# Rotary embedding on one core: runs of one position range side by side in neighbouring partitions, and nine transfers instead of ten

## The chip, the cores and the metric

The kernel runs on one core of one Trainium2 chip. The metric is the device time of an execution in microseconds, the lower the better.

## The reference

Batch 16, 512 positions, 16 heads of 64 numbers, all fp32: 33.55 MB in and as much out, both in HBM, the memory outside the core. Only the first 32 numbers of each head change.

```python
x1, x2 = x[..., :32], x[..., 32:]
cos, sin = cos[None, :, None, :], sin[None, :, None, :]     # from [512, 32]
first  = x1[..., :16] * cos[..., :16] - x1[..., 16:] * sin[..., :16]
second = x1[..., :16] * sin[..., :16] + x1[..., 16:] * cos[..., :16]
out = concatenate([first, second, x2], axis=-1)
```

## The kernel before

x is cut into four tiles of four batches. A tile has 128 partitions (the rows of the on-chip memory), and each partition holds a run of K = 16 positions, 64 KiB in one piece. The on-chip ring holds three tiles, so load 3 must wait until store 0 has emptied its slot. All large transfers are issued by SyncE into one queue, in program order. Partition p holds run p of the tile's four batches in memory order, that is position range p mod 32, so the small tables (32 ranges) are copied four times.

```python
    xf = x.rearrange("b s h d -> (b s h d)").rearrange("(t p f) -> t p f", t=T, p=P)
    ...
    def load(t, lo=0, hi=K):
        nc.sync.dma_start(out=rows(t, lo, hi), in_=xf[t, :, lo * R : hi * R])
    ...
    nc.gpsimd.dma_start(out=stage[:, 0].rearrange("p k j -> p (k j)"), in_=cosf)
    nc.gpsimd.dma_start(out=stage[:, 1].rearrange("p k j -> p (k j)"), in_=sinf)
    load(0, 0, K0)          # K0 = 4 rows
    load(0, K0, K)
    load(1)
    load(2, 0, KC)          # KC = 8 rows
    for r in range(REP):    # REP = 4
        nc.vector.tensor_copy(out=table[r * PB : (r + 1) * PB]..., in_=stage...)
    ...
    def rotate(t, lo, hi):  # four VectorE instructions on rows lo to hi
        ...
    rotate(0, 0, K0)
    rotate(0, K0, (K0 + K) // 2)
    rotate(0, (K0 + K) // 2, K)
    store(0)
    load(2, KC, K)
    load(3)
    for t in range(1, T):
        rotate(t, 0, KC)
        rotate(t, KC, K)
        store(t)
```

## Time and profile before

| | before |
|---|---|
| time, median | 161.92 us (161.79 to 162.01, 6 runs) |
| span in the profile | 160.1 us |
| VectorE busy | 110.0 us |
| large transfers' queue | 97.8% of 16 engines' span |

The span runs from the first to the last instruction. A share near 100% says that the 16 transfer engines always had work; idle time of VectorE costs nothing then. The main lines are in the prediction. An issue is the instruction that hands a transfer over; a transfer lands when the last of its 16 engines has reported.

### The profile page before, as it was taken

The page shows a single profiled execution, that of the slowest core. Times are in us where ns is not written, and L with a number is a line of the kernel's source. Part 1 is how long each engine was busy: PE and PEld are TensorE (multiplying, and loading weights), DVE is VectorE, ACT ScalarE, POOL GpSimd, SP SyncE. Part 2 cuts the span into 40 slices and gives each one's busy share as a digit, 9 for nine tenths or more (in the row PEclk, how much of TensorE's full clock was granted, in tenths as well). Part 3 has the DMA queues.
Part 4 walks back from the last instruction along what each step waited for, and adds up shares of the span by engine and source line. Part 5 has one row for each costly group of instructions (what it writes and reads, how often), then busy time and mean ns, then how long its engine had stood idle before and what let it go on. Part 6 is the DMA issues. An engine that isn't in the chain of part 4 may idle for free.

```text
span 160.1 us, 109 instructions
## 1 busy us (share of the span) xinstructions
DVE 110.0 (69%) x40; POOL 1.3 (1%) x6
## 2 busy tenths in 40 slices
DVE  0069709999999999999999994799999900000000
POOL 3000000000000000000000000000000000000000
DMA  6999999699699799899996996996996996996991
GB/s 197 385 504 454 393 459 524 262 524 491 295 401 581 328 524 409 377 393 418 483 540 295 491 524 262 524 524 262 524 524 262 524 524 262 524 491 295 524 459 66
DMA packets 1504, 67.24 MB, mean 420 GB/s; under 512 B 192, under 2 KB 192, under 8 KB 224
## 3 DMA queue, kind: packets, MB, share of 16 engines
q1 hardware_dynamic: 1440, 67.11, 97.8%
q0 software_dynamic: 64, 0.13, 0.2%
HBM read 33.69 MB, written 33.55 MB: 420 GB/s over the span
## 4 chain that ended last, share of the span: by engine, by line
DMA 50%; DVE 28%; DVEq 1%; issue 0%; SPq 0%
DMA ring<-in_x_dram 32%; DMA out_dram<-ring 18%; DVE b_t L83 10%; DVE ring L84 10%; DVE ring L85 5%; DVE ring L88 3%; DVEq L127 1%; SPq L53 0%; DVEq L83 0%
## 5 line engine op out<-in xcount | busy, mean ns | idle before, releaser
L83 DVE TENSOR_TENSOR b_t<-ring,table 128x4096 f32<-128x4096 f32 (+2 forms) x9 | 35.6, 3959 | 8.2 <-DMA ring<-in_x_dram 8.0
L84 DVE TENSOR_TENSOR ring<-ring,table 128x4096 f32<-128x4096 f32 (+2 forms) x9 | 35.6, 3950 | 0.3
L85 DVE TENSOR_TENSOR ring<-ring,b_t 128x2048 f32<-128x2048 f32 (+2 forms) x9 | 18.4, 2049 | 0.3
L88 DVE TENSOR_TENSOR ring<-ring,b_t 128x2048 f32<-128x2048 f32 (+2 forms) x9 | 18.4, 2042 | 0.0
L67 DVE COPY table<-stage 32x1024 f32<-32x1024 f32 x4 | 2.7, 684 | 9.2 <-DMA stage<-in_sin_dram 9.1
L58 POOL DMA_DIRECT2D stage<-in_cos_dram x1 | 0.6, 631 | 0.8 <-PEq L127 0.8
L59 POOL DMA_DIRECT2D stage<-in_sin_dram x1 | 0.5, 498 | 0.0
L116 POOL MEMSET const-bfloat16-1.0<- 128x1 bf16 x1 | 0.1, 102 | 0.0
L116 POOL MEMSET const-float32-0.0<- 128x1 f32 x1 | 0.1, 99 | 0.2 <-issue 0.2
L116 POOL MEMSET const-float32-1.0<- 128x1 f32 x1 | 0.1, 99 | 0.0
L116 POOL MEMSET const-uint8-127<- 128x1 uint8 x1 | 0.1, 99 | 0.0
## 6 DMA issues: line engine op xcount, KB each, us to landing
ring<-in_x_dram SPq DMA_DIRECT2D x2, 4096.0 KB, 43.9
ring<-in_x_dram SPq DMA_DIRECT2D x1, 6144.0 KB, 22.4
ring<-in_x_dram SPq DMA_DIRECT2D x1, 2048.0 KB, 8.5
stage<-in_cos_dram POOLq DMA_DIRECT2D x1, 64.0 KB, 6.0
stage<-in_sin_dram POOLq DMA_DIRECT2D x1, 64.0 KB, 7.2
out_dram<-ring SPq DMA_DIRECT2D x4, 36.4
ring<-in_x_dram SPq DMA_DIRECT2D x2, 35.0
```

Source lines behind the costliest of these rows:

```text
L58: nc.gpsimd.dma_start(out=stage[:, 0].rearrange("p k j -> p (k j)"), in_=cosf)
L59: nc.gpsimd.dma_start(out=stage[:, 1].rearrange("p k j -> p (k j)"), in_=sinf)
L67: nc.vector.tensor_copy(out=table[r * PB : (r + 1) * PB].rearrange("p t k c j -> p (t k) c j"), in_=stage.rearrange("p t k j -> p (t k) j" ...
L83: nc.vector.tensor_mul(out=b_t, in0=x1, in1=s)
L84: nc.vector.tensor_mul(out=x1, in0=x1, in1=c)
L85: nc.vector.tensor_sub(out=x1[:, :, :, 0:Q], in0=x1[:, :, :, 0:Q], in1=b_t[:, :, :, Q:HF])
L88: nc.vector.tensor_add(out=x1[:, :, :, Q:HF], in0=x1[:, :, :, Q:HF], in1=b_t[:, :, :, 0:Q])
L116: nc = _bacc.Bacc("TRN2", target_bir_lowering=False, num_devices=1)
L127: with _tile.TileContext(nc) as tc:
```

## The change

Partition 4j+b now holds range j of batch b. Four neighbouring partitions need the same table row, so one shuffle, whose mask names a source for each of 32 partitions, replaces the four copies. The transfers are regrouped: three whole loads, two stores, the last load in 7 and 9 rows, two stores.

```diff
-    xf = x.rearrange("b s h d -> (b s h d)").rearrange("(t p f) -> t p f", t=T, p=P)
+    xf = x.rearrange("(t b) (j k) h d -> t j b (k h d)", t=T, k=K)
     ... (of alike)
-        nc.sync.dma_start(out=rows(t, lo, hi), in_=xf[t, :, lo * R : hi * R])
+        nc.sync.dma_start(out=rows(t, lo, hi), in_=xf[t, :, :, lo * R : hi * R])
     ...
+    nc.vector.memset(stage[:, :, :, 0:Q], 0.0)
+    first = stage.rearrange("(j b) t k i -> j b t (k i)", b=REP)
+    nc.gpsimd.dma_start(out=first[:, 0, 0], in_=cosf)     # every fourth partition
     ...
-    load(0, 0, K0)
-    load(0, K0, K)
+    load(0)
     load(1)
-    load(2, 0, KC)
+    load(2)
-    for r in range(REP):
-        nc.vector.tensor_copy(...)
+    nc.vector.stream_shuffle(out=table..., in_=stage..., mask=[p // REP * REP for p in range(32)])
     ...
-    rotate(0, 0, K0)
-    rotate(0, K0, (K0 + K) // 2)
-    rotate(0, (K0 + K) // 2, K)
-    store(0)
-    load(2, KC, K)
-    load(3)
-    for t in range(1, T):
+    for t in range(NS - 1):
         rotate(t, 0, KC)
         rotate(t, KC, K)
         store(t)
+    load(NS, 0, KA)         # KA = 7
+    load(NS, KA, K)
+    for t in range(NS - 1, T):
+        cuts = [0, KC, K] if t < NS else [0, KA, (KA + K) // 2, K]
+        for lo, hi in zip(cuts, cuts[1:]):
+            rotate(t, lo, hi)
+        store(t)
```

More of the change, by code (lines that the diff above doesn't have):

```diff
@@ L33 @@
     KC = K // 2
-    K0 = K // 4
-    xf = x.rearrange("b s h d -> (b s h d)").rearrange("(t p f) -> t p f", t=T, p=P)
-    of = out.rearrange("b s h d -> (b s h d)").rearrange("(t p f) -> t p f", t=T, p=P)
+    KA = 7
+    xf = x.rearrange("(t b) (j k) h d -> t j b (k h d)", t=T, k=K)
+    of = out.rearrange("(t b) (j k) h d -> t j b (k h d)", t=T, k=K)
     cosf = cos.rearrange("(p k) j -> p (k j)", k=K)
@@ L45 @@
     ring = const_pool.tile([P, NS, K, H, D], fp32)
-    stage = const_pool.tile([PB, 2, K, HF], fp32)
+    stage = const_pool.tile([P, 2, K, HF], fp32)
     table = const_pool.tile([P, 2, K, 2, Q], fp32)
@@ L52, in load @@
     def load(t, lo=0, hi=K):
-        nc.sync.dma_start(out=rows(t, lo, hi), in_=xf[t, :, lo * R : hi * R])
+        nc.sync.dma_start(out=rows(t, lo, hi), in_=xf[t, :, :, lo * R : hi * R])
     def store(t, lo=0, hi=K):
-        nc.sync.dma_start(out=of[t, :, lo * R : hi * R], in_=rows(t, lo, hi))
-    nc.gpsimd.dma_start(out=stage[:, 0].rearrange("p k j -> p (k j)"), in_=cosf)
-    nc.gpsimd.dma_start(out=stage[:, 1].rearrange("p k j -> p (k j)"), in_=sinf)
-    load(0, 0, K0)
-    load(0, K0, K)
-    load(1)
-    load(2, 0, KC)
-    for r in range(REP):
-        nc.vector.tensor_copy(
-            out=table[r * PB : (r + 1) * PB].rearrange("p t k c j -> p (t k) c j"),
-            in_=stage.rearrange("p t k j -> p (t k) j")[:, :, 0:Q]
-            .unsqueeze(2)
-            .to_broadcast((PB, 2 * K, 2, Q)),
-        )
+        nc.sync.dma_start(out=of[t, :, :, lo * R : hi * R], in_=rows(t, lo, hi))
+    nc.vector.memset(stage[:, :, :, 0:Q], 0.0)
+    first = stage.rearrange("(j b) t k i -> j b t (k i)", b=REP)
+    nc.gpsimd.dma_start(out=first[:, 0, 0], in_=cosf)
+    nc.gpsimd.dma_start(out=first[:, 0, 1], in_=sinf)
+    load(0)
+    load(1)
+    load(2)
+    nc.vector.stream_shuffle(
+        out=table.rearrange("p t k c j -> p (t k) c j"),
+        in_=stage.rearrange("p t k j -> p (t k) j")[:, :, 0:Q]
+        .unsqueeze(2)
+        .to_broadcast((P, 2 * K, 2, Q)),
+        mask=[p // REP * REP for p in range(32)],
+    )
     C = table[:, 0].rearrange("p k c j -> p k (c j)")
@@ L76, in rotate @@
     def rotate(t, lo, hi):
-        n = hi - lo
         x1 = ring[:, t % NS, lo:hi, :, 0:HF]
-        c = C[:, lo:hi].unsqueeze(2).to_broadcast((P, n, H, HF))
-        s = Sn[:, lo:hi].unsqueeze(2).to_broadcast((P, n, H, HF))
+        c = C[:, lo:hi].unsqueeze(2).to_broadcast((P, hi - lo, H, HF))
+        s = Sn[:, lo:hi].unsqueeze(2).to_broadcast((P, hi - lo, H, HF))
         b_full = b_pool.tile([P, KC, H, HF], fp32, name="b_t")
-        b_t = b_full[:, 0:n]
+        b_t = b_full[:, 0 : hi - lo]
         nc.vector.tensor_mul(out=b_t, in0=x1, in1=s)
```

## The prediction

> **What bounds the kernel now.** I read the page first, its parts 1 to 3. In this page the columns are shares of the span or, in the rows of digits, tenths busy in 40 slices of 4 us.
>
> ```profile
> span 160.1 us, 109 instructions
> DVE 110.0 (69%) x40; POOL 1.3 (1%) x6
> DVE  0069709999999999999999994799999900000000
> DMA  6999999699699799899996996996996996996991
> q1 hardware_dynamic: 1440, 67.11, 97.8%
> HBM read 33.69 MB, written 33.55 MB: 420 GB/s over the span
> ```
>
> The reader is to see that VectorE is busy for 69% and the transfers for 97.8 + 0.2%. The queue moved 67.11 MB in 0.978 x 160.1 = 156.6 us, or 429 GB/s while it worked. Each byte of x is read once and each byte of the output written once, so no change of layout makes the bytes fewer. The slices with 6 are an effect of counting large packets where they end, as longer windows show.
>
> Next, windows longer than a packet (columns: window, its length, VectorE busy, POOL busy, clock, DMA share, GB/s), and three short ones at the two ends.
>
> ```profile
> 54.00:100.00 46.00, 43.59 (x14) 0.00 (x0) 1.00 1.00 433
> 2.00:158.00 156.00, 110.01 (x40) 0.38 (x1) 1.00 1.00 430
> 1.00:1.50 0.50, 0.00 (x0) 0.25 (x1) 1.00 0.00 0
> 1.50:2.00 0.50, 0.00 (x0) 0.50 (x2) 1.00 2.12 459
> 159.00:159.50 0.50, 0.00 (x0) 0.00 (x0) 1.00 0.00 0
> ```
>
> From 2 to 158 us the share is 1.00: there is no hole to fill. What lies outside is the start (first bytes between 1.5 and 2.0 us, for a load issued at 0.74) and about 1.5 us at the end.
>
> Third, the time from issue to landing of single transfers, which I asked for in narrow windows, and the chain of waits from store 0 on.
>
> ```profile
> ring<-in_x_dram SPq DMA_DIRECT2D x1, 41.3
> out_dram<-ring SPq DMA_DIRECT2D x1, 28.2
> ring<-in_x_dram SPq DMA_DIRECT2D x1, 28.8
> out_dram<-ring SPq DMA_DIRECT2D x1, 47.7
> out_dram<-ring SPq DMA_DIRECT2D x1, 30.9
> ...
> 44.14 28.18 DMA out_dram<-ring
> 72.34 28.75 DMA ring<-in_x_dram
> ```
>
> These are load 1, store 0, load 3, store 1 and store 3. With their issue times (about 1.6, 44.14, 72.34, 72.77, 128.1 us in the timeline) they land at 42.9, 72.3, 101.1, 120.5 and 159.0 us. Load 3 to store 1 is 19.4 us, store 1 to store 3 is 38.5 us, two of 19.3: each 8.39 MB takes 19.35 us, whatever the direction, in the order of issue. Store 3 needs about 1 us to begin (0.74 to between 1.5 and 2.0 us for the first load), 19.35 us to move and some 0.4 us to land, 20.8 us; it took 30.9, so for 10 us it stood behind store 2. The last rotation could end 10 us later and the time would stay.
>
> **What the Trainium skill says.** "DMA: Bandwidth & Descriptors", section "Where 436 GB/s comes from", puts the ceiling of the 16 engines' ports at 435.2 GB/s. The trace agrees: 433 GB/s from 54 to 100 us, with loads and stores. Moving 67.24 MB at 435.2 would take 154.5 us as an estimate against 156.6 of transfer time; nobody can get over 2% here.
>
> The same page, section "Why a DMA increments its semaphore by 16 and not by 1", says that a transfer uses the largest count up to 16 that divides the slowest dimension of both sides. The new pattern in HBM is 32 runs by 4 batches by 16384 elements, against 128 partitions; 16 divides 32 and 128. All engines stay in use. No run yet shows it for this pattern.
>
> Its section "Latency and other measured facts" lists copies that slow down at row pitches of large powers of two (207 GB/s per direction at 512 KiB, 164 at 2 MiB). The new layout brings a 2 MiB step between batches, but partitions that follow one another in run j are 64 KiB apart for a fixed batch. The trace of before, with a pitch of 64 KiB throughout, is at the ceiling and shows no such loss.
>
> "VectorE: DVE Perf Modes", section "The perf-mode tier table (the rule you actually need)", lets an fp32 copy run two elements a cycle, and tensor_tensor and STREAM_SHUFFLE one. The trace agrees for the first two: 32x1024 copies take 0.684 us, a 128x1024 tensor_tensor 1.220 us.
>
> **The change, part by part.** The tables: four copies of 0.684 us go, 2.74 us. One shuffle of 128x1024 comes, at the one-element rate as long as the tensor_tensor of that size, 1.22 us. A memset of 128x512 comes; by the slope of the tensor_tensor rows (2048 elements 2.301 us, 4096 in 4.433: 1.04 ns each and 0.17 fixed) at most 0.7 us. VectorE thus goes from 110.0 to about 109.2 us. None of it is on the path: the memset lies before the tables' transfers are issued, near 1.3 us, and the shuffle ends before 12 us, while the first whole load lands after 23 us.
>
> The first load: before, 4 of its 16 rows landed at 9.2 us and VectorE began rotating at 11.94. Now it must wait for all 16. The two loads of before had the same bytes and the second landed at 23.57, so the whole one lands at 23.5. I use the cadence of the rows before: 8 rows every 13.45 us (44.15, 57.60, 71.04), 6 rows in 10.24; so by a straight line 7 rows 11.85, 4 rows 7.04, 5 rows 8.64. Rotation 0 runs 23.6 to 50.5, rotation 1 to 77.4, rotation 2 to 104.3. Before, they ended at 44.1, 71.0 and 97.9: VectorE is 6.4 us late, and the idle time that it had in front moves.
>
> The queue: loads 0, 1 and 2 land at 23.5, 42.8 and 62.1. Store 0 is issued at 50.5, over 10 us before the data of load 2 ends, and lands at 81.6. Store 1 is issued at 77.4; store 0's data ends near 81, less 1 us to begin, so it is in time by about 2.5 us. Load 3 reuses the buffer of store 0 and can be issued at 81.7, long before store 1's data ends near 100. Its first part (7/16 of 19.35 us, 8.5) lands at 109.5, the second at 120.3. Store 2, issued at 104.3, lands at 139.7. VectorE stands idle from 104.3 to 109.6, turns 7 rows until 121.4, finds the second part landed, and ends at 128.5 and 137.1. Store 3 is issued there.
>
> Store 2's data ends some 0.4 to 0.9 us before its landing, engine by engine, near 139.0. Store 3 can have begun by 138.1. So it is in time, with 10 us of slack shrunk to about 1. It ends at 139.7 + 19.3 = 159.0, as before.
>
> Fewer transfers: two loads were split before, one now. Halving a load costs little: 9.7 us is the step from load 1 to the half load 2 (50.5 us after about 2.2, 52.7), against 19.35 / 2 = 9.68. Within the accuracy of these views a split is worth 0.1 to 0.2 us, so one fewer gives about 0.1 us.
>
> The sum: tables 0, late start 0 (absorbed by 10 us of slack), one split fewer -0.1, hence a span of 160.0 us and a time of 161.8.
>
> **The rivals.** First, the late end of VectorE becomes the bound. Margins of 2.5 us at store 1 and about 1 us at store 3 speak for it, since a start latency of 2 us in place of 1, or a rotation 1 us longer, opens a hole at the queue. Against it: all durations come from the same shapes in this trace. It would cost what it overruns, 0.5 to 1.5 us: 162.3 to 163.3. I give it one chance in five.
>
> Second, the new order in HBM changes the rate. The change may be made so that engines read neighbouring runs together. For a gain there is no room: 433 against a ceiling of 435 is 0.7 us at most, 161.1. For a loss, 2 MiB steps between batches; a drop of 3% would make it 166.5. Each engine works through large packets of whole 64 KiB rows, and the packet-by-packet timing of before shows no trouble with large strides. I give a loss of over 2% some 3 or 4 in 100.
>
> Third, the tables come late, since their transfers now wait for the memset, and their destination is every fourth partition. They landed about 9 us in and are wanted at 23.5; they would have to be 11 us later to matter. Dismissed.
>
> Fourth, shortening VectorE by 0.8 us pays. Its slack says no: nothing.
>
> **Range and chances.** The bytes and the rate set 161.8 within 0.2. The second rival's gain lowers it to 161.2 and the first rival's hole lifts it to 162.6; that is the range. Within 2% is 158.7 to 165.1. Faster by that would need more than the ceiling: 1%. Slower needs a layout loss: 4%. The same: 95%.
>
> **What would show it.** A DMA share of 1.00 from 2 to 158 us and a hardware queue near 97.7%. Whole transfers 19.35 us apart. The chain of waits no longer goes back from the last rotation straight to store 0 at 44 us only, but through rotation 0 as well: load 0 to 23.5, VectorE to 50.5, store 0 to 81.6, load 3's first part to 109.5, VectorE to 137.1, store 3 to the end. Store 3 takes 21 to 22 us from issue to landing instead of 30.9. One gap of some 5 us on VectorE before the seven rows. I am wrong if the DMA share drops in a window around 138 us (the first rival) or if transfers are more than 19.5 us apart (the second).

## More of the kernel before

One view which the prediction did not use became important: the issue instructions on SyncE, by line (duration in ns as least, median and most, then first and last start in us). Line 53 is the loads, 56 the stores.

```profile
L53 SPq DMA_DIRECT2D ring<-in_x_dram x6: 327/425/504, 0.7 to 72.3; - x6
L56 SPq DMA_DIRECT2D out_dram<-ring x4: 332/346/378, 44.1 to 128.1; - x4
```

An issue took 0.35 to 0.43 us.

## The result and the profile after

The changed kernel took 163.24 us (median of 6, 162.46 to 163.91), against 161.92. The ratio is 1.0078, 95% interval 1.0051 to 1.0106. Ratios here are the mean time of one kernel's fast runs over that of the other's of the same rounds, so not quite the ratio of the medians. It is the same within 2%, yet slower clear of noise, by 1.3 us, and above the range's upper end of 162.6. It also scatters over 1.4 us, where before scatters over 0.2.

The profiled execution is the quickest of the six, 162.46 us. Its page, parts 1 to 3, answers line by line to the first lines of the prediction:

```profile
span 160.7 us, 107 instructions
DVE 109.1 (68%) x39; POOL 1.4 (1%) x6
q1 hardware_dynamic: 1296, 67.11, 97.2%
HBM read 33.69 MB, written 33.55 MB: 418 GB/s over the span
```

VectorE is at 109.1 us (109.2 was predicted) and the bytes are the same. Windows (columns as in the prediction):

```profile
54.00:100.00 46.00, 45.62 (x15) 0.00 (x0) 1.00 1.00 430
2.00:158.00 156.00, 108.57 (x38) 0.88 (x2) 1.00 1.00 431
1.50:2.00 0.50, 0.00 (x0) 0.30 (x1) 1.00 0.00 0
2.00:2.50 0.50, 0.00 (x0) 0.50 (x2) 1.00 3.81 1180
```

The share is 1.00 again: no hole. But between 1.5 and 2.0 us, where before already moved bytes, nothing moves. (A packet is booked at its start, so the short window in which nine packets of 64 KiB begin shows an impossible rate. The prediction has it the other way round, "counting large packets where they end"; its use of longer windows stands.) The chain of waits (start, length, what) and the time from issue to landing of store 3, in us:

```profile
0.73 22.95 DMA ring<-in_x_dram
...
50.66 31.70 DMA out_dram<-ring
...
82.38 27.76 DMA ring<-in_x_dram
...
136.34 1.40 DVEq L130
```

```profile
out_dram<-ring SPq DMA_DIRECT2D x1, 21.9
```

Two more times from issue to landing, of load 1 (the median of the three whole loads) and of load 2:

```profile
ring<-in_x_dram SPq DMA_DIRECT2D x3, 41.6
ring<-in_x_dram SPq DMA_DIRECT2D x1, 60.9
```

Load 1 was issued at 1.45 us and load 2 at 2.08, so they landed at 43.03 and 62.97, 19.94 us apart.

The chain above is the one that the prediction named: load 0, VectorE from 23.7 to 50.66, store 0, the first part of load 3, VectorE to 137.7, store 3. All of it runs 0.2 us late at the first link and 0.6 to 0.8 us late from store 0 on. The groups of the new VectorE instructions (count, busy us, mean ns, idle before):

```profile
L69 DVE STREAM_SHUFFLE table<-stage 128x1024 f32<-128x1024 f32 x1 | 1.3, 1286 | 0.0
L59 DVE MEMSET stage<- 128x512 f32 x1 | 0.5, 485 | 0.9 <-PEq L119 0.9
```

Finally the issue instructions, loads and stores:

```profile
L54 SPq DMA_DIRECT2D ring<-in_x_dram x5: 583/603/1110, 0.7 to 83.0; - x5
L57 SPq DMA_DIRECT2D out_dram<-ring x4: 569/596/606, 50.7 to 137.8; - x4
```

They take 0.60 us instead of 0.35 to 0.43 (medians), with fewer of them. The first load's own issue took 0.667 us, against 0.383.

**A sum for the queue.** The trace also records each packet's start and duration. Of the large packets (8 KiB and more, so without those of the tables) I take the 16 earliest starts (one for each engine), the sum of all durations divided by 16 ("work"), and the 16 latest ends. For each execution: mean start + work + holes = mean end, and mean end + unequal end = the last end. The time was 3.1 to 3.25 us more than the last end in every trace below but e8's (3.4). The records do not name the engine. The sum splits up the end of an execution; it doesn't say by itself which term caused which.

### The profile page after: what moved, and what is told of

Same layout as the page of the kernel before. It is cut to its first block, busy times and chain, and to the rows that moved or that the text cites. A ratio compares the mean times of both kernels' runs of the same rounds, so it can differ in the third digit from the quotient of the medians.

```text
span 160.7 us, 107 instructions
## 1 busy us (share of the span) xinstructions
DVE 109.1 (68%) x39; POOL 1.4 (1%) x6
## 4 chain that ended last, share of the span: by engine, by line
DMA 51%; DVE 31%; issue 2%; DVEq 1%
DMA ring<-in_x_dram 32%; DMA out_dram<-ring 20%; DVE b_t L85 11%; DVE ring L86 11%; DVE ring L90 5%; DVE ring L87 4%; DVEq L130 1%; DVEq L85 0%
## 5 line engine op out<-in xcount | busy, mean ns | idle before, releaser
L85 DVE TENSOR_TENSOR b_t<-ring,table 128x4096 f32<-128x4096 f32 (+3 forms) x9 | 35.6, 3958 | 12.0 <-DMA ring<-in_x_dram 11.7
L86 DVE TENSOR_TENSOR ring<-ring,table 128x4096 f32<-128x4096 f32 (+3 forms) x9 | 35.6, 3950 | 0.3
L87 DVE TENSOR_TENSOR ring<-ring,b_t 128x2048 f32<-128x2048 f32 (+3 forms) x9 | 18.4, 2050 | 0.3
L90 DVE TENSOR_TENSOR ring<-ring,b_t 128x2048 f32<-128x2048 f32 (+3 forms) x9 | 18.4, 2043 | 0.0
L69 DVE STREAM_SHUFFLE table<-stage 128x1024 f32<-128x1024 f32 x1 | 1.3, 1286 | 0.0
L59 DVE MEMSET stage<- 128x512 f32 x1 | 0.5, 485 | 0.9 <-PEq L119 0.9
```

Source lines behind the costliest of these rows:

```text
L59: nc.vector.memset(stage[:, :, :, 0:Q], 0.0)
L69: nc.vector.stream_shuffle(out=table.rearrange("p t k c j -> p (t k) c j"), in_=stage.rearrange("p t k j -> p (t k) j")[:, :, 0:Q] .unsque ...
L85: nc.vector.tensor_mul(out=b_t, in0=x1, in1=s)
L86: nc.vector.tensor_mul(out=x1, in0=x1, in1=c)
L87: nc.vector.tensor_sub(out=x1[:, :, :, 0:Q], in0=x1[:, :, :, 0:Q], in1=b_t[:, :, :, Q:HF])
L90: nc.vector.tensor_add(out=x1[:, :, :, Q:HF], in0=x1[:, :, :, Q:HF], in1=b_t[:, :, :, 0:Q])
```

## The experiments

At the start I had four theories. M: store 3 comes too late, so VectorE's margin is gone and the queue has a hole (the prediction's first rival). L: the new order of rows in HBM makes transfers stumble. S, later called P: issuing the new pattern is slower and the first bytes are late. W, added later: the first store stalls the queue. Each group of four shared its runs of before, whose medians were 162.07 and, in the second and third group, 161.94 us.

**e0_after_again.** The changed kernel, unaltered.

> The changed kernel, unaltered, for a second trace and more times. All theories: about 163.2 us, between 162.4 and 164. Theory M (the margin of store 3 is gone, so the queue runs dry before it): where this execution is slower than 162.5 us the trace shows store 3 landing more than 19.5 us after store 2, by as much as the execution is slower. Theory L (the new order of rows in HBM gives transfers that stumble at random): store 3 follows store 2 by 19.3 us, and the excess lies in other transfers that are over 19.5 us apart. Theory S (a slower start of each transfer with the three-level pattern in HBM) explains about 0.4 us at the start and no spread by itself.

163.05 us, ratio 1.0057 (1.0041 to 1.0073). The traced execution was one of the longer ones, 163.32 us, yet store 3 landed at 160.56, 19.3 us after store 2 at 141.25. M falls. First bytes at 2.17 us. Load 2 landed 20.4 us after load 1, one step over 19.5.

**e1_layout_only.** New order of partitions and shuffle, with the transfers and cuts of before.

```diff
-    load(0)
+    load(0, 0, K0)
+    load(0, K0, K)
     ... (the rest of the schedule as in the kernel before)
```

> New partition order, memset and shuffle, but the ten transfers and the cuts of before. Theory M: the 10 us of slack are back, so 161.9 to 162.4 us with a spread under 0.3 us. Theory L: 163.0 us or more with a spread of 1 us. Theory S: first bytes 0.3 to 0.5 us later than before, 162.2 to 162.4 us, and an issue instruction of 0.6 us against 0.4.

163.16 us, ratio 1.0072 (1.0057 to 1.0087): the layout alone does nearly all. First bytes at 2.17 us, issues at 0.60 us. The half load 2 landed 11.2 us after load 1; 9.7 was the step before. So S had the first bytes and the issue right, but its time (162.2 to 162.4) was too short; the time is the one that L named.

**e2_schedule_only.** The nine transfers in the old order, with four copies.

```diff
     ... (kernel before)
-    load(0, 0, K0)
-    load(0, K0, K)
+    load(0)
     ... (the rest of the schedule as in the changed kernel)
```

> Nine transfers and the cuts of the changed kernel, but the partition order and the four copies of before. Theory M: the margin of store 3 is about 1 us less the start of a transfer, as in the prediction, so 161.8 to 163 us, and what it is over 162 shows as a gap between stores 2 and 3. Theory L: 161.7 to 162.0 us with little spread. Theory S: first bytes at about 1.75 us as before, and an issue of 0.4 us.

162.29 us, ratio 1.0011 (0.9998 to 1.0024), not clear of noise. First bytes at 1.74 us, with the same whole 64 KiB rows as the changed kernel. Load 2 still landed 19.8 us after load 1, and no hole stood before store 3. So the nine transfers are about free, as predicted. The issues of its loads and stores:

```profile
L53 SPq DMA_DIRECT2D ring<-in_x_dram x5: 339/426/647, 0.7 to 82.4; - x5
L56 SPq DMA_DIRECT2D out_dram<-ring x4: 343/344/348, 50.4 to 137.5; - x4
```

**e3_early_rows.** The changed kernel with load 0 in 4 and 12 rows.

```diff
-    load(0)
+    load(0, 0, 4)
+    load(0, 4, K)
     ... (rotation 0 in 4, 6 and 6 rows)
```

> The changed kernel with its first load split in 4 and 12 rows and rotation 0 in 4, 6 and 6 rows, as before, so that VectorE ends rotation 2 about 6 us earlier; the wait for the last load is unchanged, so VectorE still ends near 137.5 us. Theory M: no gain, since the last rotation starts at the landing of load 3's first part whatever came before: 163 us. If instead the late stores 0 and 1 are what hurts, 162.2 us. Theory L: 163 us with spread. Theory S: 162.3 us if the whole 64 KiB rows of the first load were what delayed the first bytes (then they come at 1.75 us), 163 us otherwise.

163.12 us, ratio 1.0066 (1.0041 to 1.0090). A smaller first transfer doesn't bring the first bytes forward (2.19 us), and an earlier VectorE, whose store 0 was issued at 44.0 instead of 50.7, gains nothing.

**e4_stores_as_before** and **e5_loads_as_before.** Only loads, or only stores, use the new order. Their outputs are wrong, which doesn't matter for the times. The edit of e4, and e5 is its mirror image:

```diff
-    of = out.rearrange("(t b) (j k) h d -> t j b (k h d)", t=T, k=K)
+    of = out.rearrange("b s h d -> (b s h d)").rearrange("(t p f) -> t p f", t=T, p=P)
     ... (index of the store to match)
```

> Wrong on purpose: the loads keep the new order of rows, the stores go out in the old order, so rows end in the wrong place. Theory P (the three-level pattern makes an issue slower and the first bytes later): issue of a load 0.6 us, of a store 0.35, first bytes at 2.2 us. Theory W (the first store in the new order stalls the queue): the step from load 1's landing to load 2's falls to 19.9 us or less, as in the run with the old order, and the time is about 162.6 us. If instead the loads do all the harm, 163 us.

> Wrong on purpose: loads in the old order, stores in the new one. Theory P: issue of a load 0.35 us, of a store 0.6, first bytes at 1.75 us, so 162.6 to 162.8 us at most. Theory W: the step from load 1 to load 2 stays at 20 to 20.8 us.

With new loads (e4): 163.06 us, ratio 1.0059 (1.0044 to 1.0074), first bytes at 2.12 us. With old loads (e5): 162.60 us, ratio 1.0036 (1.0024 to 1.0049), first bytes at 1.76. The issue follows the pattern, transfer by transfer; first e4's loads and stores, then e5's loads and stores, and e5's window at the start:

```profile
L54 SPq DMA_DIRECT2D ring<-in_x_dram x5: 566/596/849, 0.7 to 83.1; - x5
L57 SPq DMA_DIRECT2D out_dram<-ring x4: 333/338/344, 50.6 to 137.9; - x4
```

```profile
L54 SPq DMA_DIRECT2D ring<-in_x_dram x5: 334/417/550, 0.7 to 82.5; - x5
L57 SPq DMA_DIRECT2D out_dram<-ring x4: 544/548/630, 50.1 to 137.6; - x4
...
1.50:2.00 0.50, 0.00 (x0) 0.29 (x1) 1.00 4.33 1442
```

Both keep the memset and the shuffle, so those are not the cause of the late start. The new loads alone make the whole loss, as e4's last alternative said. But the new stores (with the new tables) and early first bytes still cost about half of it, so the late start isn't all. W's forecast for e4 failed: load 2 came 20.2 us after load 1 in e4 and 20.3 in e5.

**e6_warm_store.** The changed kernel with a small store to the output at the very start, from ScalarE.

```diff
+    warm = const_pool.tile([P, 128], fp32)
+    nc.vector.memset(warm, 0.0)
+    nc.scalar.dma_start(out=of[0, :, :, 0:128], in_=warm)
     load(0)
```

> The changed kernel with a store of 128 zeros per partition to the same rows of the output at the very start, overwritten later, so correct. If the stall ahead of store 0 belongs to the first access to the output, it goes: load 2 lands 19.4 us after load 1 instead of 19.9 to 20.8, and the time falls by 0.5 to 1 us, to about 162.4. If it belongs to the turn from reading to writing, the step stays and the time is 163.1 to 163.3.

163.18 us, ratio 1.0078 (1.0059 to 1.0098), load 2 20.4 us after load 1: nothing gained. An early small access to these rows does not remove the stall.

**e7_halves.** A different order, 64 runs by 2 halves. Its output is wrong, which doesn't matter for the time.

```diff
-    xf = x.rearrange("(t b) (j k) h d -> t j b (k h d)", t=T, k=K)
+    xf = x.rearrange("b s h d -> (b s h d)").rearrange("(t h i f) -> t i h f", t=T, h=2, i=P // 2)
     ... (of alike)
```

> Wrong on purpose (the tables don't fit): another three-level pattern, 64 runs by 2 halves that are 4 MiB apart, for loads and stores. Theory P: issue 0.6 us and first bytes at 2.2 us again, and so at least 162.5 us, as the levels and not the addresses count. A theory of addresses: first bytes at another time than 2.2, or a step from load 1 to load 2 that is clearly different, under 19.6 or over 21 us.

162.83 us, ratio 1.0047 (1.0033 to 1.0062). Other addresses, the same issue and the same late first bytes:

```profile
L54 SPq DMA_DIRECT2D ring<-in_x_dram x5: 588/606/962, 0.7 to 82.8; - x5
...
1.50:2.00 0.50, 0.00 (x0) 0.30 (x1) 1.00 0.00 0
2.00:2.50 0.50, 0.00 (x0) 0.50 (x2) 1.00 5.55 1835
```

So the late start goes with the form of the pattern, not with the particular addresses.

**e8_flat.** The changed kernel with every transfer cut into four, one for each batch.

```diff
-        nc.sync.dma_start(out=rows(t, lo, hi), in_=xf[t, :, :, lo * R : hi * R])
+        for b in range(REP):
+            nc.sync.dma_start(out=rows(t, lo, hi)[b::REP], in_=xf[t, :, b, lo * R : hi * R])
     ... (store alike)
```

> The changed kernel, every transfer cut into four of one batch each, so that the pattern in HBM has two levels (32 runs of 64 KiB) and the addresses stay those of the change; correct. Theory P (levels of the pattern): issue back to 0.35 us, first bytes at 1.75 us instead of 2.2. If only the levels hurt, the time falls to 162.3 us like the schedule alone; if the addresses are to blame for the rest (unequal engines), only the 0.4 us at the start come back, 162.7 us.

A failed experiment as to the time: 270.96 us. With partitions taken in steps of four, the waits became far stricter (rotation 0 began at 62.8 us, only after load 2, and the next product waited for store 0), which I had not looked for. Two things can still be read. The issue was not quicker:

```profile
L55 SPq DMA_DIRECT2D ring<-in_x_dram x20: 468/594/1394, 0.7 to 155.4; - x20
```

and first bytes came at 2.08 us, so two levels in HBM with a partition step of four on chip are slow too; theory P in its strict form, levels in HBM alone, is not right. And where the queue had run dry before the last stores, the 16 engines ended within 0.14 us of each other, 0.09 us from mean to last, closer than in any other trace.

**e9_before_again.** The kernel before, for a second trace.

> The kernel before, for a second trace: 161.9 us. It tells whether its lack of a stall ahead of the first store (72.32 for store 0 after 52.64 for the half load 2, 19.7 us) is the rule: 19.5 to 19.8 us again, and the half load 2 at 9.7 us after load 1. If the stall comes at random in all kernels, 10.2 us or more from load 1 to the half load 2 here, at an unchanged end.

162.03 us, ratio 1.0005 (0.9992 to 1.0018). The half load 2 landed 9.7 us after load 1 and store 0 19.9 us after that.

**e10_warm_sp.** The small store put into SyncE's queue after load 0.

```diff
     ... (warm made as in e6)
     load(0)
+    nc.sync.dma_start(out=of[0, :, :, 0:128], in_=warm)
     load(1)
```

> The changed kernel with a small store (512 bytes per partition, overwritten later) in the same queue between loads 0 and 1; correct. If the stall is that of the queue's first turn from reading to writing, it moves to the small store near 22 us and load 2 lands 19.4 us after load 1, the time unchanged at 163.1 us or up to 0.7 us less. If it needs a large first store, load 2 still lands 19.9 to 20.8 us after load 1, and the time is 163.2 to 163.5 us.

163.15 us, ratio 1.0076 (1.0062 to 1.0091). Load 2 came 20.1 us after load 1: a small first turn to writing in the same queue doesn't take the stall away.

**e11_tables_act.** The kernel before with its tables issued by ScalarE.

```diff
-    nc.gpsimd.dma_start(out=stage[:, 0]...
+    nc.scalar.dma_start(out=stage[:, 0]...
     ... (sin alike)
```

> The kernel before with its two table transfers issued by ScalarE instead of GpSimd. In the trace of before, rows of the first load took up to 0.34 us longer while the tables came (0.64 us per engine from 4 to 20 us). If that is the work of the tables' queue, up to 0.5 us faster than before, 161.4 to 161.7 us; if it is the first load's own, 161.9 us.

162.09 us, ratio 1.0006 (0.9993 to 1.0018): no gain. Packets of the first 20 us were held up less (0.84 us per engine over the plain 2.418 us per 64 KiB, against 1.30), but now the last packets ahead of store 0 were held up by 0.62 us, against 0.10. In all, held-up time was 1.61 us against 1.64. That is a warning about theory W: a stall at one place is not yet a cost.

**Four more traces.** What stayed open was whether the transfer work or unequal engines carry the scatter. These are single executions, so of unknown state.

> The changed kernel. If late and unequal engines are the cause: mean start of the 16 engines 2.3 to 2.6 us, transfer work per engine 156.1 to 156.7 us as before, holes under 0.15 us, and the last engine 0.5 to 1.1 us after the mean end, with the time following that sum to 0.1 us. If the work is the cause: over 157 us of work in a slow execution.

> As for the third trace of the changed kernel: the sum of mean start, work, holes and unequal end predicts the time to 0.1 us, and the differences between executions come mainly from the unequal end.

> The kernel before: mean start 1.9 us, work 156.4 us, unequal end 0.2 to 0.4 us, 161.8 to 162.1 us.

> Nine transfers in the old order: mean start 1.9 to 2.0 us, work 156.4 to 156.7 us, unequal end 0.3 to 0.5 us, 161.9 to 162.5 us.

The forecasts of the sum held to about 0.1 us, and work stayed under 157 us in the slowest execution. All traces but e8's, with the terms of the sum in us:

| trace | mean start | work | holes | unequal end | last end | time |
|---|---|---|---|---|---|---|
| before | 1.88 | 156.40 | 0.10 | 0.22 | 158.60 | 161.85 |
| e9, before | 1.90 | 156.45 | 0.13 | 0.38 | 158.86 | 162.02 |
| f3, before | 1.87 | 156.42 | 0.10 | 0.41 | 158.80 | 161.98 |
| e2, new schedule only | 1.92 | 156.68 | 0.12 | 0.45 | 159.16 | 162.29 |
| f4, new schedule only | 1.97 | 156.53 | 0.14 | 0.28 | 158.92 | 162.13 |
| e1, new layout only | 2.34 | 156.85 | 0.14 | 0.56 | 159.89 | 163.05 |
| after | 2.58 | 156.11 | 0.10 | 0.54 | 159.34 | 162.46 |
| f1, after | 2.38 | 156.61 | 0.12 | 0.69 | 159.80 | 162.91 |
| e0, after | 2.36 | 156.68 | 0.12 | 1.04 | 160.20 | 163.32 |
| f2, after | 2.45 | 156.49 | 0.15 | 1.33 | 160.43 | 163.54 |
| e3, early rows | 2.39 | 156.80 | 0.14 | 0.97 | 160.30 | 163.45 |
| e4, new loads only | 2.46 | 156.50 | 0.10 | 0.55 | 159.62 | 162.73 |
| e5, new stores only | 2.03 | 156.79 | 0.10 | 0.58 | 159.50 | 162.61 |
| e6, warm store | 2.48 | 156.54 | 0.37 | 1.33 | 160.73 | 163.90 |
| e7, halves | 2.35 | 156.52 | 0.10 | 0.30 | 159.27 | 162.40 |
| e10, warm store in SyncE's queue | 2.35 | 156.52 | 0.31 | 0.73 | 159.90 | 163.08 |
| e11, tables from ScalarE | 2.01 | 156.36 | 0.13 | 0.47 | 158.96 | 162.07 |

The means of the three traces of before are 1.88 + 156.42 + 0.11 + 0.34 = 158.75, and the mean time is 161.95. Those of the four of after are 2.44 + 156.47 + 0.12 + 0.90 = 159.94 (terms rounded), and the mean time 163.06. Of 1.19 us at the last end, 0.56 are the late start, 0.56 the unequal end, 0.05 work and 0.01 holes. The four times of after stand in the order of the unequal end, which spreads over 0.79 us of the 1.08 us between them; the work does not set that order, as the quickest and the slowest execution have 156.11 and 156.49 us and the two between them more.

(In e6 and e10 the small store's packets count as holes.) The mean start falls into two groups without overlap: 2.34 to 2.58 us in the ten traces with the loads in a new order, 1.87 to 2.03 in the seven with the old one. The unequal end doesn't divide so cleanly: e7 has new loads and 0.30, e5 old loads and 0.58. And e1, e3 and e5 have over 0.3 us more work than before, which the means of after hide.

## Why the prediction was wrong

The steps that held. The transfers bound both kernels, and the mean work per engine is the same to 0.05 us, so neither the fear nor the hope of the second rival, a changed rate in HBM, came true. The Trainium skill ("DMA: Bandwidth & Descriptors", "Latency and other measured facts") lists 164 GB/s per direction for copies between HBM tensors with 2 MiB from partition to partition. Here four neighbouring partitions lie 2 MiB apart, and no such loss shows: 430 GB/s from 54 to 100 us. All 16 engines were in use: 64 KiB took an engine 2.418 us, and 16 times that rate is 434 GB/s. The tables and VectorE cost nothing on the path; memset and shuffle took 0.49 and 1.29 us. The tables landed later than I had supposed, at 16.4 us instead of about 9, and still 7 us early. The first rival, a hole at store 3, did not happen: holes are 0.10 to 0.15 us in all four traces of after, though the margin did shrink to 21.9 us from issue to landing. That 163.24 us lies inside the 162.3 to 163.3 which I gave this rival is chance; and my range, up to 162.6, left out most of what I had given it. (One small sum is off, without effect: 62.1 + 19.35 is 81.45, not the 81.6 given for store 0.) The new schedule alone came out at 1.0011, as the sum said.

The step that failed is the sum of the queue, "It ends at 139.7 + 19.3 = 159.0, as before". It rests on load 0 being in the queue as early as before ("The two loads of before had the same bytes and the second landed at 23.57, so the whole one lands at 23.5") and on the engines ending no further apart than before. Any change in these two had the size zero in my sum, and both were missing from the range. By the landings, the first link that is clearly off is load 2: predicted for 62.1 us, it landed at 62.97 to 63.45 in the four traces of after, 19.94 to 20.36 us after load 1. So a sign of being wrong that I had named, transfers more than 19.5 us apart, did appear, though not by a lower rate: in the profiled execution every other whole transfer followed the one before it by 19.28 to 19.39 us.

First, the start: 0.56 us on average over the engines. The first bytes come at 2.17 to 2.19 us instead of 1.75 to 1.77, and the last engine begins at 3.1 to 3.6 us instead of 2.0 to 2.1. e4, e5 and e7 show that it goes with the form of the pattern of the loads, and the first issue is longer in the same cases (0.61 to 0.67 against 0.38 to 0.39 us; in the two profiled kernels that is 0.28 of the 0.44 us); e3 shows that a smaller first load doesn't help. Why the bytes come later by more than the issue is not shown. Nor is it shown that this delay itself reaches the end. Averaged over the engines, load 1 landed at 42.58 to 42.66 us in the traces of after and at 42.50 to 42.76 in those of before: the late start had been made up. Packets that began between 5 and 20 us were held up by 0.43 to 0.65 us per engine in before and by 0.00 in after (held up: longer than 2.418 us per 64 KiB). That saving goes with the new tables: 0.00 to 0.09 us in the eleven traces of the table with them, e5's old loads included, and 0.30 to 0.86 in the six with the old ones. In this mean, after falls behind only between load 1 and load 2.

Second, the unequal end: 0.90 us instead of 0.34. The first landings of after were already 0.8 to 1.0 us apart from the first to the last engine (before: under 0.5 at load 0), and the spread was still there at the end. e8 fits this: after the queue had run dry it was all but gone. That an engine late at the start stays late because it never waits was my reading, and the traces speak against it in that form: from the mean start to the last start it is 1.04 us in the profiled execution and 0.66 in f2, whose unequal ends are 0.54 and 1.33, and f4 starts with 0.82 and ends with 0.28. What goes along with the unequal end is how far apart the engines are when load 0 lands (0.79 to 0.81 us in the two quicker traces of after, 0.97 to 0.98 in the two slower). Why the spread grows further in some executions, from 1.2 to 1.7 us at the second part of load 3 in f2, stays open.

The stall ahead of store 0 is real, 0.55 to 0.91 us of held-up packets per engine in the four traces of after (0.04 to 0.28 in the three of before), and it is where after falls behind. Yet by the sum it only takes the place of what before lost between 5 and 20 us. f4 had 0.03 there and 0.86 in the first 20 us after the ramp, e11 and e2 had it in the old order, and the work in total stays within 156.1 to 156.9 us. What moves it about is not settled. So it is shown that the new layout costs the time, and that new loads begin late; how much of the 1.1 us is due to the late start stays open.

## What to carry to other kernels

When transfers bound a kernel from the first byte to the last, look at the two ends of the queue as well: ask when the first bytes come, and how evenly the engines end. Here a layout that made the pattern of each transfer more involved had its first bytes 0.44 us later, and the longer issue instruction showed it. Give a range room for such terms whenever a change rewrites the pattern of the first transfer, even if the bytes and row lengths stay.

## What the Trainium skill lacked or had wrong

- "DMA: Bandwidth & Descriptors", "Latency and other measured facts", gives about 600 ns to the first byte of a transfer issued from SyncE. It doesn't say from where it counts. Here it was about 1.0 us from the start of the issue with the plain pattern (0.74 to 1.75 us) and about 1.45 with the new one (0.73 to 2.19); from the end of the issue it was 0.63 and 0.79 us.
- The same page has no figure for how the pattern's form changes the issue on this chip: 0.34 to 0.43 us against 0.55 to 0.61 us (medians; 0.70 for the loads of e10), for 128 rows.
- No page gives a figure for how far apart the engines of one queue begin and end: 0.90 us from mean to last end here, 0.34 us in the kernel before.
- The same page, "Queues, rings and completion order", says that engines alternate between queues packet by packet. The trace agrees: the tables' first packets, of data and of completion, begin 2.57 us apart, which leaves room for one packet of 64 KiB (2.418 us). And it adds a cost: the tables, in a second queue, landed at 9.0 us where the first load began with packets of 16 KiB (before and e3) and at 16.1 to 16.4 us where it began with packets of 64 KiB (e2 and after).
- "VectorE: DVE Perf Modes", "Zero memsets can be issued as uint32 (trn2)", gives a memset one cycle per element. At the page's 0.96 GHz, 512 elements would be at least 0.53 us as an estimate; the 128x512 fp32 memset took 0.485 us.
